# A two-layer hybrid encoder on one core: wider tiles for GLA's v, the gates' low-rank columns taken with retention's v, and another iteration for inverse roots

## The chip, the cores and the metric

The kernel runs on one core of one Trainium2 chip. The time is that of one execution on the device in microseconds, given as the median of several runs. The trace is of one execution of its own, and its terms are added up against that execution's time.

## The reference, cut to what matters

Two layers over 512 tokens of 1024 channels. In each, a normalized input h is projected to all branches at once; three mixers (retention, an S5 state space model, gated linear attention, GLA) work side by side, are gated and merged, and an MLP follows. What the change touches, from the reference:

```python
h = rmsnorm(x, norm1_g[l])
z = h @ w_in[l]
a_q, a_k, a_v, a_g, b_u, c_q, c_k, c_v, c_lr, c_r = jnp.split(z, split_idx, axis=-1)
...
ro = retention_bidir(rq, rk, a_v.reshape(Bn, L, RET_HEADS, RET_DV))
...
la_f = (jax.nn.log_sigmoid(lr @ gla_w_gate[l, 0].astype(jnp.float32)
                           + gla_b_gate[l, 0].astype(jnp.float32)) / GLA_TAU
        ).reshape(Bn, L, GLA_HEADS, GLA_DK)
...
go_f = gla_chunked(gq, gk, gv, la_f, False)
```

a_v has 256 columns (retention's v), c_v has 512 (GLA's v), and c_lr has 16, the low-rank input lr of GLA's forget gates. Inverse square roots stand in every RMSNorm and in the norms of the heads of GLA and retention.

## The kernel before, in words

Precision is kept by splitting: every float32 operand of a large matmul becomes a rounded part ("hi") and a rest ("lo"), and a product is three matmuls (hi by hi, hi by lo, lo by hi). Weights come from memory in chunks of 128 x 1024, two layers of 128 chunks; `weights` (L99) loads a chunk on SP's queue into one of three "raw" buffers, casts it on ScalarE (whi, L112) and subtracts on VectorE (wlo, L113), into a ring of five buffers. `col_tile` (L120 to L132) makes 128 output channels by 512 tokens from one chunk: 8 blocks of rows times 3 matmuls of 512 columns (L129 to L131).

h itself is not normalized before the projection: each result is scaled by the inverse root when it is evicted, as a row R over tokens or, for v, as a column r of 128 tokens.

`layer` (L311) sets the order in which the work is traced: the two u tiles of S5 (in layer 0 `u_first`, made while x arrives); `lr_proj` (L485), 16 matmuls of 512 columns that give lr with the tokens along the row; four q and k tiles of GLA, each copied twice per head by DMA ("dup", L327); the gates (`gla_gate`, L521); GLA's v by two calls of `v_tiles` (L275), each 256 columns wide; GLA's states and reads; four rotary tiles of retention (`z_tile`, `rotary`, with copies "rsw" L641 and "qfb" L672); retention's v, a third call of `v_tiles`, centred by `center` (L647); retention; then tiles of silu and merge gates, between which S5 is worked off in steps ("bg"). A step of S5 is set behind the latest product of retention's q on GpSimd (L674) and behind instructions of the tile just made (`bg_steps`). Then come the branch projections, the output projection and the MLP; at the end the last 512 tokens are done in two halves of 256, so that one half is normalized while the other is multiplied (`emit_out`).

In `v_tiles` h is the stationary side and the weights are streamed: four token tiles share two PSUM banks, and each of the 96 matmuls is 256 columns wide (L288, L290, L292). PSUM has four banks tagged "mm" (large products) and four tagged "ms" (small ones).

`rsqrt` (L134) makes an inverse root on VectorE: a shift, a multiply-add on the integer view, and three Newton steps of three instructions.

This order is not the final one: a planner takes the traced instructions, the priorities given by `hp`, the edges given by `issue_after`, a cost model and the free on-chip memory, writes each engine's queue, and chooses how many buffers a tag without a fixed count gets. Each engine then runs its queue strictly in order.

## Time and profile before

| | us |
|---|---|
| runs shown | 1573.23, 1573.24, 2206.6 |
| median | 1573.24 |
| profiled execution | 1574.72 |
| its span, first to last instruction | 1572.6 |
| TensorE busy in it | 1546.8 |

The span leaves out 2.1 us around the instructions. A line such as "PE L129 MATMUL mm<-hh,whi 128*128 128x512" is line 129's matmul with a 128 x 128 stationary side and 512 streamed columns, into the PSUM tile mm, from hh (the hi part of h) and whi. PE is TensorE, DVE VectorE, ACT ScalarE, POOL GpSimd, SP the engine that issues most DMAs. In brackets stands the engine's idle time just before, and what ended it. PEclk is the granted share of TensorE's full clock.

### The profile page before, as it was taken

What the parts mean: (1) busy time and instruction counts of PE and PEld (TensorE: products, weight loads), DVE (VectorE), ACT (ScalarE), POOL (GpSimd) and SP (SyncE); (2) the same over time, 40 slices, a digit from 0 to 9 for tenths busy, and PEclk for the clock granted to TensorE, in tenths of its full rate; (3) what the DMA queues carried; (4) which work ended last, traced back from release to release, by engine and by line L of the source; (5) the groups of instructions that cost most, each with busy time, mean ns of one, the idle gap of its engine ahead of it and who ended that gap; (6) DMA issues with size and microseconds to landing.
All of it is one profiled execution on the core that took longest, in us unless ns stands there. A gap on an engine that the chain in (4) does not pass through costs nothing.

```text
span 1572.6 us, 20692 instructions
## 1 busy us (share of the span) xinstructions
PE 1546.8 (98%) x8118; PEld 1289.1 (82%) x8118; DVE 934.1 (59%) x1583; ACT 567.8 (36%) x853; POOL 204.4 (13%) x327
## 2 busy tenths in 40 slices
PE   9999999999999999999999999999999999999997
PEld 6888877788888888888889888788888888888897
DVE  6786999855556657434548889744455434344353
ACT  5533333243433332423335324332343423232342
POOL 8242010141200000000101210102111000000002
PEclk9999999999999999999999999999999999999999
DMA  6424222233323223232434322333242223323221
GB/s 209 148 65 124 86 75 89 91 108 126 121 100 103 97 93 100 94 108 94 147 116 140 108 68 81 95 98 103 94 139 102 94 94 103 99 94 108 94 94 54
DMA packets 60512, 163.36 MB, mean 104 GB/s; under 512 B 10556, under 2 KB 17212, under 8 KB 60416
## 3 DMA queue, kind: packets, MB, share of 16 engines
q1 hardware_dynamic: 60096, 161.01, 31.5%
q8 instruction: 64, 1.05, 0.3%
q0 software_dynamic: 320, 1.05, 0.2%
q14 instruction: 32, 0.26, 0.1%
HBM read 147.11 MB, written 6.52 MB: 98 GB/s over the span
## 4 chain that ended last, share of the span: by engine, by line
PE 81%; DVE 11%; DMA 2%; issue 2%; SPq 2%; POOL 1%; ACT 1%; DVEq 0%; POOLq 0%; ACTq 0%
PE mm L129 24%; PE mm L131 24%; PE mm L130 24%; DVE wlo L113 2%; PE mm L290 1%; PE mm L292 1%; PE mm L288 1%; DMA rsw<-za 1%; DVE g L372 1%; DMA dup<-zc 1%; DMA s5y<-yscr 0%; DMA raw<-wst 0%; SPq L1111 0%; SPq L641 0%; PE ms L701 0%
## 5 line engine op out<-in xcount | busy, mean ns | idle before, releaser
L113 DVE TENSOR_TENSOR wlo<-raw,whi 128x1024 fp32r<-128x1024 f32 (+1 forms) x258 | 325.1, 1261 | 273.0 <-PE mm L130 198.2
L112 ACT CAST whi<-raw 128x1024 fp32r<-128x1024 f32 (+1 forms) x258 | 266.7, 1044 | 542.2 <-PE mm L131 437.0
L131 PE MATMUL mm<-hh,wlo 128*128 128x512 f32 x1136 | 445.9, 393 | 1.5 <-DVE wlo L113 1.5
L129 PE MATMUL mm<-hh,whi 128*128 128x512 f32 x1136 | 446.1, 393 | 0.0
L130 PE MATMUL mm<-hl,whi 128*128 128x512 f32 x1136 | 444.7, 391 | 0.0
L131 PEld LDWEIGHTS mm<-hh,wlo 128*128 128x128 f32 x1136 | 213.6, 188 | 47.8 <-DVE wlo L113 3.0
L129 PEld LDWEIGHTS mm<-hh,whi 128*128 128x128 f32 x1136 | 213.6, 188 | 45.8 <-issue 2.3
L130 PEld LDWEIGHTS mm<-hl,whi 128*128 128x128 f32 x1136 | 213.6, 188 | 44.7 <-issue 1.1
L130 PE MATMUL mm<-fl,whi 128*128 128x512 f32 (+1 forms) x576 | 210.7, 366 | 0.0
L131 PE MATMUL mm<-fh,wlo 128*128 128x512 f32 (+1 forms) x576 | 210.2, 366 | 0.0
L129 PE MATMUL mm<-fh,whi 128*128 128x512 f32 (+1 forms) x576 | 209.5, 366 | 0.0
L130 PEld LDWEIGHTS mm<-fl,whi 128*128 128x128 f32 x576 | 108.6, 189 | 17.7
L129 PEld LDWEIGHTS mm<-fh,whi 128*128 128x128 f32 x576 | 108.6, 189 | 17.7
L131 PEld LDWEIGHTS mm<-fh,wlo 128*128 128x128 f32 x576 | 108.6, 189 | 17.5
L182 POOL TENSOR_TENSOR acc<-acc,sq 128x512 f32<-128x512 f32 (+1 forms) x30 | 32.5, 1085 | 564.2 <-ACT sq L181 564.2
L118 DVE TENSOR_TENSOR fl<-ht,fh 128x512 fp32r<-128x512 f32 x64 | 44.3, 692 | 76.9 <-ACT fh L117 76.8
L446 ACT ACTIVATE ht<-ht 128x512 f32<-128x512 f32 x64 | 40.4, 631 | 86.0 <-DVE ht L445 86.0
L373 ACT ACTIVATE g<-g,cst 128x512 f32<-128x512 f32 x48 | 34.7, 724 | 88.4 <-DVE g L372 88.4
L471 DVE TENSOR_TENSOR x<-x,mm 128x512 f32<-128x512 f32 x56 | 38.3, 683 | 44.8 <-PE mm L131 44.8
L129 PE MATMUL mm<-y,whi 128*128 128x512 f32 x160 | 62.6, 391 | 0.8 <-DVE s5Y L1105 0.8
L130 PE MATMUL mm<-y,whi 128*128 128x512 f32 x160 | 62.6, 392 | 0.0
L131 PE MATMUL mm<-y,wlo 128*128 128x512 f32 x160 | 62.2, 390 | 0.0
(265 smaller groups left out, 1944.2 us busy)
## 6 DMA issues: line engine op xcount, KB each, us to landing
raw<-wst SPq DMA_DIRECT2D x254, 512.0 KB, 3.3
dup<-zc SPq DMA_DIRECT2D x32, 128.0 KB, 3.5
rsw<-za SPq DMA_DIRECT2D x32, 64.0 KB, 2.0
qfb<-za SPq DMA_DIRECT2D x16, 128.0 KB, 3.4
x<-xT SPq DMA_DIRECT2D x8, 256.0 KB, 3.6
xs<-x SPq DMA_DIRECT2D x8, 256.0 KB, 3.9
x<-xs SPq DMA_DIRECT2D x8, 256.0 KB, 3.8
outT<-out SPq DMA_DIRECT2D x8, 256.0 KB, 2.7
```

Source lines behind the costliest of these rows:

```text
L112: nc.scalar.copy(hi[:, s], raw[:, s])
L113: nc.vector.tensor_sub(lo[:, s], raw[:, s], hi[:, s].bitcast(F32))
L118: self.nc.vector.tensor_sub(lo, src, hi.bitcast(F32))
L129: nc.tensor.matmul(ps, hi[:, o:o + P], a, start=first and k == 0, stop=False)
L130: nc.tensor.matmul(ps, hi[:, o:o + P], b, start=False, stop=False)
L131: self.mmi = nc.tensor.matmul(ps, lo[:, o:o + P], a, start=False, stop=last and k == n - 1)
L182: return (eng or (nc.vector if j == KT - 1 else nc.gpsimd)).tensor_add(accs[0], accs[0], t)
L288: nc.tensor.matmul(o, a[:, s], hi[:, k * 256:(k + 1) * 256], start=f, stop=False, skip_group_check=True)
L290: nc.tensor.matmul(o, a[:, s], lo[:, k * 256:(k + 1) * 256], start=False, stop=False, skip_group_check=True)
L373: act = nc.scalar.activation(g, g, AF.Sigmoid, bias=self.smc(l, SM_BM, j))
L446: act = nc.scalar.square(t, t)
L471: ev = nc.vector.tensor_add(self.x[j], self.x[j], ps)
```

## The change

Three things are done. GLA's v is made by `v_wide`: four chunks of 256 rows by 512 columns, each token tile in a bank of its own, 96 matmuls of 512 columns. Retention's v is made by `v_lr` together with the 16 columns of lr, 272 columns in all, in two chunks of 128 x 1088, and ahead of GLA's q and k; `lr_rows` scales lr per token, splits it side by side, transposes it in four pieces and gives the gates 50 rows to contract over instead of 98. All buffers of raw and split weights become 1088 wide. Inverse roots take one Newton step and one step of third order, nine instructions in place of eleven. The host's layout of weights follows (two unused chunks are left in the numbering).

```diff
@@ -22,6 +22,8 @@
+LW = 1088
+LC = 2
@@ -105,10 +107,11 @@
             bufs = dict(bufs=5) if tag == "w" else {}
-            hi = self.sb.tile([P, CW], F32R, tag=tag, name=self.nm("whi"), **bufs)
-            lo = self.sb.tile([P, CW], F32R, tag=tag, name=self.nm("wlo"), **bufs)
+            hi = self.sb.tile([P, LW], F32R, tag=tag, name=self.nm("whi"), **bufs)
+            lo = self.sb.tile([P, LW], F32R, tag=tag, name=self.nm("wlo"), **bufs)
+            cw = self.width(c)
             for i in range(n):
-                s = slice(CW // n * i, CW // n * (i + 1))
+                s = slice(cw // n * i, cw // n * (i + 1))
                 nc.scalar.copy(hi[:, s], raw[:, s])
@@ -139,10 +142,14 @@
         u = self.small(shape, tag + "u")
-        for _ in range(3):
-            nc.vector.scalar_tensor_tensor(u, y, -0.5, y, ALU.mult, ALU.mult)
-            nc.vector.tensor_mul(u, u, v)
-            nc.vector.scalar_tensor_tensor(y, u, 1.5, y, ALU.add, ALU.mult)
+        c = math.sqrt(0.375)
+        nc.vector.scalar_tensor_tensor(u, y, -0.5, y, ALU.mult, ALU.mult)
+        nc.vector.tensor_mul(u, u, v)
+        nc.vector.scalar_tensor_tensor(y, u, 1.5, y, ALU.add, ALU.mult)
+        nc.vector.scalar_tensor_tensor(u, y, -c, y, ALU.mult, ALU.mult)
+        nc.vector.tensor_mul(u, u, v)
+        nc.vector.scalar_tensor_tensor(u, u, 1.25 / c, u, ALU.add, ALU.mult)
+        nc.vector.scalar_tensor_tensor(y, u, 1.875, y, ALU.add, ALU.mult)
         return y
@@ -231,12 +238,17 @@
+    def width(self, c):
+        return LW if LC <= c < LC + 2 else CW
-        raw = self.sb.tile([P, CW], F32, tag="raw", bufs=3, name=self.nm("raw"))
+        raw = self.sb.tile([P, LW], F32, tag="raw", bufs=3, name=self.nm("raw"))
+        cw = self.width(c)
+        src = self.io["wst"][l, c] if cw == CW else self.io["wlr"][l, c - LC]
-            s = slice(CW // n * i, CW // n * (i + 1))
-            dma = self.nc.sync.dma_start(raw[:, s], self.io["wst"][l, c][:, s])
+            s = slice(cw // n * i, cw // n * (i + 1))
+            dma = self.nc.sync.dma_start(raw[:, s], src[:, s])
@@ -272,31 +284,51 @@
-    def v_tiles(self, l, h, r):
-        nc = self.nc
-        ps = [self.mm([P, 2, 256]) for _ in range(2)]
+    def v_lr(self, l, h, r):
+        nc = self.nc
+        ps = [f([P, 272]) for f in (self.mm, self.mm, self.ms, self.ms)]
         for half in range(2):
             for tt in range(4):
-                o = ps[tt // 2][:, tt % 2, :]
+                s = slice(tt * P, (tt + 1) * P)
                 for k in range(4):
                     a, b = h[half * 4 + k]
-                    s = slice(tt * P, (tt + 1) * P)
-                    f = half == 0 and k == 0 and tt % 2 == 0
-                    e = half == 1 and k == 3 and tt % 2 == 1
-                    nc.tensor.matmul(o, a[:, s], hi[:, k * 256:(k + 1) * 256], start=f, stop=False,
-                                     skip_group_check=True)
-                    nc.tensor.matmul(o, a[:, s], lo[:, k * 256:(k + 1) * 256], start=False, stop=False,
-                                     skip_group_check=True)
-                    nc.tensor.matmul(o, b[:, s], hi[:, k * 256:(k + 1) * 256], start=False, stop=e,
-                                     skip_group_check=True)
+                    wh, wl = (w[:, k * 272:(k + 1) * 272] for w in (hi, lo))
+                    nc.tensor.matmul(ps[tt], a[:, s], wh, start=half == 0 and k == 0, stop=False)
+                    nc.tensor.matmul(ps[tt], a[:, s], wl, start=False, stop=False)
+                    nc.tensor.matmul(ps[tt], b[:, s], wh, start=False, stop=half == 1 and k == 3)
         out = []
+        lr = self.slot(shape=(P, 4, 16), s="lr")
         with self.hp(15000):
                     out.append(self.slot(shape=(P, 2, 256), s="v"))
-                nc.scalar.activation(out[-1][:, tt % 2, :], ps[tt // 2][:, tt % 2, :], AF.Copy, scale=r[:, tt:tt + 1])
+                rr = r[:, tt:tt + 1]
+                nc.scalar.activation(out[-1][:, tt % 2, :], ps[tt][:, 0:256], AF.Copy, scale=rr)
+                nc.scalar.activation(lr[:, tt, :], ps[tt][:, 256:272], AF.Copy, scale=rr)
+        return out, lr
+    def v_wide(self, l, h, r):
+        nc = self.nc
+        ps = [self.mm() for _ in range(4)]
+        for c in range(4):
+            hi, lo = self.weights(l)
+            for tt in range(4):
+                s = slice(tt * P, (tt + 1) * P)
+                for k in range(2):
+                    a, b = h[2 * c + k]
+                    wh, wl = (w[:, k * 512:(k + 1) * 512] for w in (hi, lo))
+                    nc.tensor.matmul(ps[tt], a[:, s], wh, start=c == 0 and k == 0, stop=False)
+                    nc.tensor.matmul(ps[tt], a[:, s], wl, start=False, stop=False)
+                    nc.tensor.matmul(ps[tt], b[:, s], wh, start=False, stop=c == 3 and k == 1)
+        out = []
+        with self.hp(15000):
+            for tt in range(4):
+                out.append(self.slot(s="v"))
+                nc.scalar.activation(out[-1], ps[tt], AF.Copy, scale=r[:, tt:tt + 1])
         return out
@@ -315,7 +347,8 @@
         us = [self.u_tile(l, h, R, ps) for ps in pu]
-        lrT = self.lr_proj(l, h, R)
+        av, lr = self.v_lr(l, h, r)
+        lrT = self.lr_rows(l, lr)
         qd, kd = [], []
@@ -328,7 +361,7 @@
             gl = [self.gla_gate(hd, lrT, qd[hd], kd[hd]) for hd in range(4)]
-        cv = [self.v_tiles(l, h, r) for _ in range(2)]
+        cv = self.v_wide(l, h, r)
         if l == 0:
@@ -350,7 +383,7 @@
                     lst.append(self.rotary(z, cs, sn))
-        av = self.center(self.v_tiles(l, h, r))
+        av = self.center(av)
         with self.hp(8000):
@@ -482,40 +515,31 @@
-    def lr_proj(self, l, h, R):
+    def lr_rows(self, l, lr):
         nc, io = self.nc, self.io
-        with self.hp(20000):
-            raw = self.slot(s="wlr")[:, 0:KT * 16].rearrange("p (k c) -> p k c", c=16)
-            with self.tc.issue_after(self.wdma.ins):
-                nc.sync.dma_start(raw, io["wlr"][l])
-            w = self.sb.tile([P, KT, P], F32R, tag="w", bufs=5, name=self.nm("wlrs"))
-            nc.gpsimd.memset(w.bitcast(F32), 0.0)
-            self.wcp = nc.scalar.copy(w[:, :, 0:16], raw)
-            nc.vector.tensor_sub(w[:, :, 16:32], raw, w[:, :, 0:16].bitcast(F32))
-        ps = self.mm()
-        for k in range(KT):
-            nc.tensor.matmul(ps, w[:, k, :], h[k][0], start=k == 0, stop=False)
-            nc.tensor.matmul(ps, w[:, k, :], h[k][1], start=False, stop=k == KT - 1)
         lrT = self.slot(F32R, s="lrT")
         with self.hp(15000):
-            t = self.slot(s="lrt")
-            nc.vector.tensor_mul(t[0:32, :], ps[0:32, :], R[0:32, :])
-            nc.scalar.copy(lrT[0:32, :], t[0:32, :])
-            nc.vector.tensor_sub(lrT[32:64, :], t[0:32, :], lrT[0:32, :].bitcast(F32))
-            self.lrc = nc.scalar.copy(lrT[64:96, :], t[0:32, :])
-            with self.tc.issue_after(self.uev.ins):
-                nc.vector.memset(lrT[96:128, :].bitcast(F32), 1.0)
+            t = self.slot(shape=(P, 4, 64), s="lrt")
+            nc.gpsimd.memset(t[:, :, 48:64], 1.0)
+            tr = t.bitcast(F32R)
+            nc.scalar.copy(tr[:, :, 0:16], lr)
+            nc.vector.tensor_sub(tr[:, :, 16:32], lr, t[:, :, 0:16])
+            nc.scalar.copy(tr[:, :, 32:48], lr)
+            ps = self.ms()
+            for tt in range(4):
+                nc.tensor.transpose(ps[0:64, tt * P:(tt + 1) * P], t[:, tt, :], self.ident)
+            self.lrc = nc.scalar.copy(lrT[0:64, :], ps[0:64, :])
             raw = self.slot(s="wgr")
             with self.tc.issue_after(self.wdma.ins):
-                nc.sync.dma_start(raw[0:98, :], io["wg"][l])
+                nc.sync.dma_start(raw[0:50, :], io["wg"][l])
                 nc.sync.dma_start(self.scm, io["tab"][:, T_SC:T_SC + 512])
             hi = self.slot(F32R, s="wgh")
-            with self.tc.issue_after(self.wcp.ins):
-                nc.scalar.copy(hi[0:98, :], raw[0:98, :])
-            nc.vector.scalar_tensor_tensor(self.wg[0:98, :], hi[0:98, :].bitcast(F32), self.cst[0:98, C_M:C_M + 1],
-                                           raw[0:98, :], ALU.mult, ALU.add)
+            nc.scalar.copy(hi[0:50, :], raw[0:50, :])
+            nc.vector.scalar_tensor_tensor(self.wg[0:50, :], hi[0:50, :].bitcast(F32), self.cst[0:50, C_M:C_M + 1],
+                                           raw[0:50, :], ALU.mult, ALU.add)
         return lrT
@@ -523,7 +547,7 @@
         ps = self.ms()
-        nc.tensor.matmul(ps, self.wg[0:98, hd * P:(hd + 1) * P], lrT[0:98, :], start=True, stop=True)
+        nc.tensor.matmul(ps, self.wg[0:50, hd * P:(hd + 1) * P], lrT[0:50, :], start=True, stop=True)
         a = self.slot(s="a")
@@ -568,8 +592,7 @@
         nc.vector.copy_predicated(sT, self.cst[:, C_MB:C_MB + P].bitcast(U32).unsqueeze(1).to_broadcast([P, 4, P]), psb)
-        c0 = (hd % 2) * P
-        v = [cv[hd // 2][n // 2][:, n % 2, c0:c0 + P] for n in range(4)]
+        v = [x[:, hd * P:(hd + 1) * P] for x in cv]
         psk = self.ms([P, 4, P])
...
@@ -1149,11 +1172,10 @@
+        ch += [np.zeros((P, CW), f)] * 2
-        halves = lambda c: [blk(w[512 * i:512 * i + 512], c, 256) for i in range(2)]
-        ch += halves(1792) + halves(2048)
+        ch += [blk(w[256 * i:256 * i + 256], 1792, 512) for i in range(4)]
-        ch += halves(512)
```

## Rows read from the trace of the kernel before

**Rows 1.** The page's part 1: busy us of an engine, share of the span, instructions

```profile
PE 1546.8 (98%) x8118; PEld 1289.1 (82%) x8118; DVE 934.1 (59%) x1583; ACT 567.8 (36%) x853; POOL 204.4 (13%) x327
```

**Rows 2.** What TensorE waited for: us in total, times, longest

```profile
PE ms L168 <- DVE dg L166: 3.0, 1, 3.0
PE mm L131 <- DVE wlo L113: 2.1, 3, 0.9
PE ms L666 <- DVE za L644: 1.9, 1, 1.9
PE m L1101 <- DVE s5S L1080: 1.7, 1, 1.7
...
PE mm L288 <- DVE sT L570: 1.4, 1, 1.4
PE ms L959 <- DVE W L948: 1.4, 1, 1.4
```

**Rows 3.** TensorE's timeline in layer 0: start, us, line, tiles

```profile
27.51 0.39 PE L129 MATMUL mm<-hh,whi 128*128 128x512 f32 x1
...
32.72 0.39 PE L131 MATMUL mm<-hh,wlo 128*128 128x512 f32 x1
...
51.12 0.28 PE L288 MATMUL mm<-whi,hh 128*128 128x256 f32 x1
...
54.84 0.28 PE L290 MATMUL mm<-wlo,hh 128*128 128x256 f32 x1
```

**Rows 4.** Stretches: us, busy us of PE, PEld, DVE, ACT, POOL, PEclk, DMA

```profile
119.10:155.00 35.90, 33.16 (x228) 29.45 (x226) 21.61 (x36) 12.13 (x20) 6.89 (x9) 1.00 0.43 128
155.00:301.40 146.40, 143.81 (x902) 114.63 (x902) 136.22 (x300) 50.09 (x76) 20.16 (x31) 1.00 0.26 83
...
936.50:941.00 4.50, 4.50 (x20) 3.80 (x17) 3.58 (x15) 0.00 (x0) 0.00 (x0) 0.54 0.23 90
```

**Rows 5.** TensorE's timeline in layer 1, around lr_proj and four transposes

```profile
804.76 0.39 PE L497 MATMUL mm<-hh,wlrs 128*128 128x512 f32 x1
...
808.39 0.39 PE L129 MATMUL mm<-hh,whi 128*128 128x512 f32 x1
...
836.59 0.60 PE L558 MATMUL ms<-cst,dup 128*128 128x128 f32 x4
...
837.14 0.28 PE L288 MATMUL mm<-whi,hh 128*128 128x256 f32 x1
```

**Rows 6.** GLA's q and k copies: VectorE's timeline, the tile's issues and landing

```profile
50.91 0.69 DVE L545 TENSOR_TENSOR dup<-dup,cum 128x512 f32<-128x512 f32 x1 [0.76 <-ACT cum L543]
...
L327 SPq DMA_DIRECT2D dup<-zc x32: 467/594/935, 38.7 to 838.9; - x32
...
DMA to landing us min/median/max: 2.2/3.5/5.6
```

**Rows 7.** Timelines of ScalarE and of VectorE, start of layer 0

```profile
21.56 1.99 ACT L112 CAST whi<-raw 128x1024 fp32r<-128x1024 f32 x2 [2.88 <-PE mm L740]
...
24.04 2.52 DVE L113 TENSOR_TENSOR wlo<-raw,whi 128x1024 fp32r<-128x1024 f32 x2
```

**Rows 8.** Timelines of VectorE and of TensorE, end of the kernel

```profile
1563.20 0.16 DVE L143 SCALAR_TENSOR_TENSOR nu<-ny 128x2 f32<-128x2 f32 x1
...
1563.79 0.16 DVE L143 SCALAR_TENSOR_TENSOR nu<-ny 128x2 f32<-128x2 f32 x1
...
1565.00 0.90 PE L168 MATMUL ms<-dg,cst 128*128 128x256 f32 x2 [3.03 <-DVE dg L166]
```

**Rows 9.** Timelines of TensorE and GpSimd, layer 0, from retention's v on

```profile
119.10 0.40 PE L288 MATMUL mm<-whi,hh 128*128 128x256 f32 x2
...
134.39 0.40 PE L129 MATMUL mm<-hh,whi 128*128 128x512 f32 x1
...
154.96 2.52 POOL L674 TENSOR_TENSOR qfb<-qfb,cst 128x512 f32<-128x512 f32 x2 [20.20 <-DMA qfb<-za]
```

More of the change, by code (lines that the diff above doesn't have):

```diff
@@ L1133, in _layout @@
     wst = np.empty((depth, NCH, P, CW), f)
-    wlr = np.empty((depth, P, KT, 16), f)
-    wg = np.empty((depth, 98, 512), f)
+    wlr = np.empty((depth, 2, P, LW), f)
+    wg = np.empty((depth, 50, 512), f)
     s5bc = np.empty((depth, 2, P, 2, 2, 8, 16), f)
@@ L1172, in _layout @@
             wst[l, i] = c
-        wlr[l] = w[:, 2304:2320].reshape(KT, P, 16).transpose(1, 0, 2)
+        vlr = np.concatenate([w[:, 512:768], w[:, 2304:2320]], 1)
+        for i in range(2):
+            wlr[l, i] = blk(vlr[512 * i:512 * i + 512], 0, 272)
         gw, gb = A("gla_w_gate")[l], A("gla_b_gate")[l]
         gl = gw.reshape(2, 16, 4, 64).transpose(1, 2, 0, 3).reshape(16, 512)
-        wg[l, 0:96] = np.tile(gl, (6, 1))
-        wg[l, 96:98] = gb.reshape(2, 4, 64).transpose(1, 0, 2).reshape(512)
+        wg[l, 0:48] = np.tile(gl, (3, 1))
+        wg[l, 48:50] = gb.reshape(2, 4, 64).transpose(1, 0, 2).reshape(512)
         for i, (br, cr) in enumerate((("s5_b_re", "s5_c_re"), ("s5_b_im", "s5_c_im"))):
@@ L1204, in _layout @@
     cst[:, C_MB:C_MB + P] = i[:, None] > i[None, :]
-    cst[64:96, C_M] = cst[97, C_M] = -1.0
+    cst[32:48, C_M] = cst[49, C_M] = -1.0
     for hd in range(4):
```

## The prediction

> **What bounds the kernel now.** I read the page's busy times first [rows 1]: TensorE is busy for 1546.8 of 1572.6 us, VectorE for 934.1. A busy TensorE need not be at its peak, so I next listed what it waited for [rows 2]. The longest entry is 3.0 us, at the very end; the next are 1 to 2 us each. So almost the whole span is TensorE's own queue of matmuls, and a change is worth what it does to that queue, unless it opens a new wait. Third I read the pace, since a matmul's printed duration (0.39 us) overlaps the next one's: only the distance between starts counts. With 512 columns, 24 matmuls of one tile start between 27.51 and 32.72, 23 steps, 0.2265 us each; with 256 columns, 32 matmuls start between 51.12 and 54.84, 31 steps, 0.120 us each [rows 3]. Two narrow ones thus cost 0.240, one wide one 0.2265: a fixed part of about 13 ns per matmul is what widening can save. Last I looked where another engine is close to being the bound: between the last rotary tile of layer 0 (119.1) and the read of its S5 states (301.4), VectorE is busy for 21.6 of 35.9 and then for 136.2 of 146.4 us [rows 4].
>
> **Part 1, GLA's v in 512 columns.** Per layer 192 matmuls of 256 columns go (two calls of v_tiles, 96 each: three lines, four token tiles, eight blocks of rows of h), 192 x 0.120 = 23.04 us; 96 of 512 come, 96 x 0.2265 = 21.74. Gain 1.30 us per layer, all on TensorE's queue. Weight bytes, casts and splits stay the same. Four accumulators of one bank now fill all four "mm" banks for 22 us, and no head of GLA gets its v before the end of it, where heads 0 and 1 had theirs half-way. TensorE fills that time with v_wide itself and then the four rotary tiles, so I cost it at nothing; by the nearest rows, waits of the heads' mask copies [rows 2], it could be 1.4 us either way.
>
> The Trainium skill (TensorE: Matmul & The Clock Gate, Back-to-back issue gap) gives the warm step as columns / 2.4 GHz plus about 2.5 ns. By it, as an estimate, a layer's part 1 would save only 96 x 2.5 ns = 0.24 us, and the whole sum below would be 2.1 us smaller: 1567.9 in place of 1565.8. The rows show five times that fixed part in this kernel, and the measurement decides.
>
> **Part 2, the low-rank columns.** lr_proj's 16 matmuls of 512 columns go: from 804.76 to the next tile's start at 808.39, 3.63 us [rows 5]. Its memset, cast and split were done ahead and cost nothing now. In exchange, retention's 96 matmuls grow from 256 to 272 columns: between the two paces a column costs (0.2265 - 0.120) / 256 = 0.42 ns, so 96 x 16 x 0.42 ns = 0.64 us. Four transposes of 64 columns come; the nearest row is four of GLA's 128-column transposes between v matmuls, which push the second matmul behind them from 0.12 to 0.55 us after their start: 0.43 us [rows 5]. The width is the stationary side's, so I keep 0.43. The gates' four matmuls contract over 50 rows instead of 98 but still stream 512 columns: no change. Net gain 3.63 - 0.64 - 0.43 = 2.56 us per layer.
>
> VectorE loses the scaling, the split into lrT and the memset of lr and gets a smaller split and the new root's share; ScalarE gets four more evictions of 16 columns and one of the transposes. All of it stands beside the q and k tiles.
>
> **Part 3, the move.** Retention's v (two weight chunks, 48 matmuls each) now stands ahead of the four q and k tiles of GLA. Its loads on SP (512 KB each and 32 KB more for lr, whose own load of 64 KB goes) come first too, ahead of those tiles' loads and of the sixteen duplicating copies, which slip with their tiles. The q and k tiles start 96 x 0.1267 - 3.63 = 8.5 us later against the start of the layer. In layer 0 the first head's product comes at 50.91 [rows 6]. Its two tiles would now run from 27.5 + 8.5 = 36.0 to 36.0 + 48 x 0.2265 = 46.9; four copies of 0.59 us to issue and 3.5 us to land [rows 6] make it 52.8 at the earliest, 2 us late. Behind it TensorE has v_wide, which needs none of this, so I cost it at nothing; if GLA's heads end 2 us late, the rotary tiles are still in front of their readers.
>
> At layer 0's start something is uncovered. lr_proj's weights came early, and its matmuls, which by their 3.63 us began near 23.9 and ended at 27.51, hid the next chunk's cast (from 21.56, held by the u tiles, which kept the weight buffers) and its split, which began at 24.04 and took 1.26 us [rows 7]. Now that chunk is needed at 23.9 itself. Bounds: nothing, if its cast uses the buffer that lr_proj held and goes early, and 24.04 + 1.26 - 23.9 = 1.4 us, if the order stays. I take the middle, 0.7 us; in layer 1 the chunks stream and it is nothing.
>
> The buffers of weights grow from 1024 to 1088 columns, all of them. That takes on-chip memory from other tiles' buffer counts. Bounds: nothing, and a doubling of TensorE's present waits for splits, 2.1 us [rows 2]; I take nothing, as these waits are rare.
>
> **Part 4, the roots.** Eleven VectorE instructions become nine. There are 18 roots (six of norm_stats, eight of gla_read, four of retention), at 0.197 us a step (1563.20 to 1563.79 is three), so 0.39 us each and 7.1 us of VectorE in all. Only the last one is on TensorE's path: TensorE idles 3.03 us for it before 1565.00 [rows 8]. Gain 0.39 us; what is late next there is the same chain, two steps shorter. The other 17 stand beside matmuls.
>
> **The sum.** Two layers x (1.30 + 2.56) = 7.72, plus 0.39, less 0.7: 7.4 us. The profiled execution took 1574.72 us (its span and 2.1 us around it), so 1567.3; the median of the runs shown is 1.5 us under it, so I predict 1573.24 - 7.4 = 1565.8 us. That is 0.5%, well inside the 2% that a measurement of this kernel can tell from no change.
>
> **Rivals.**
>
> A, the waits of layer 0 go as well. Retention's v is now evicted and centred long before it is wanted, so its centring and two weight splits leave VectorE's queue where the rotary and S5 chains are late. The waits there, 1.9 (rotated k), 1.7 (S5 state) and 1.4 (S5 weights), sum to 5.0 us [rows 2]; in layer 1 a stretch of 4.5 us in the midst of retention ran at a granted clock of 0.54, so near the lower level, 1.2 GHz [rows 4], and may gain up to 2 us more. For it: all of these end on VectorE. Against it: the order of each queue is planned anew, and such waits appear where the plan mistimes, not where work is most. Time 1565.8 - 5.0 = 1560.8.
>
> B, slower: the move takes away S5's cover. S5's first load stands on GpSimd behind the last product of retention's q, which ended at 154.96 + 2.52 = 157.5, 38.4 us after the last rotary tile; 15.3 of these TensorE spent from 119.10 to 134.39, mostly on retention's v [rows 9]. If that chain keeps its 38.4 us while the silu tiles begin at once, S5 starts 15.3 us later against its reader, which already waits 1.7 us. VectorE's idle time in the dense stretch is 10.2 us [rows 4]; if it makes up none, all or half of that, the wait grows by 15.3, 5.1 or 10.2 us. Layer 1 has S5's tables ready and is counted as nothing. Time 1565.8 + 10.2 = 1576.0, slower than before. It decides once the slip, less what idle time recovers, is over 7.4 us. Against it: GpSimd sat idle for 20.2 us of that chain, waiting for copies [rows 9], and these can be issued earlier.
>
> C, layer 0's gain is lost: in its dense stretch VectorE sets the time, so TensorE's 3.86 us there turn into waits, and only layer 1 and the end gain. Time 1573.24 - 3.86 - 0.39 + 0.7 = 1569.7. For it: 93% busy [rows 4]. Against it: VectorE sheds work in layer 0's mixers too (7 roots x 0.39 = 2.7 us, and lr's instructions).
>
> That the change does not do what it says, with TensorE's 8118 records unchanged, I give nothing.
>
> **How the numbers follow.** Forecast 0.55, C 0.18, B 0.14, A 0.13. The forecast's own ends are its unknowns: start 0.7 either way, heads 1.4 either way, memory 0 to 2.1, so 1563.7 to 1570.0. The range for 8 in 10 takes in A and C and the near part of B (5.1 us: 1570.9, and somewhat over it): 1559.5 to 1575. Nearly all of every case is within 2% (1541.8 to 1604.7): same 0.97. Faster by over 2% would need 24 us that no row shows, 0.01; slower by over 2% would need a collapse of S5's cover in both layers, 0.02.
>
> **What would show it.** Right: TensorE's records fall by 216 (192 + 32 matmuls fewer, 8 transposes more); wide v matmuls start 0.2265 us apart and 272-column ones 0.127; no wait for lr before the gates; the last root's wait at 2.6 instead of 3.0 us. S5's load on GpSimd under 25 us after the first silu tile says C or better; over 30 says B. Wrong: TensorE idle time growing by more than 4 us between the rotary tiles and S5's read, or a granted clock under 1.0 in a new place.

## The result, and the profile of the changed kernel

The changed kernel takes 1582.87 us (median of five runs, 1579.1 to 1586.13) against 1573.24: a ratio of 1.0061, 95% interval 1.005 to 1.0072. It is 0.6% slower, where 0.5% faster had been forecast; the 7.4 us of the sum are missing and 9.6 us stand on the other side. The run of 2206.6 us of the kernel before lies far from all others and is left out of the ratio. Its profiled execution has a span of 1580.9 us, 8.3 more than before.

The busy times of the page, to be read against [rows 1]:

```profile
PE 1548.1 (98%) x7902; PEld 1278.9 (81%) x7902; DVE 919.1 (58%) x1541; ACT 579.1 (37%) x853; POOL 199.7 (13%) x327
```

TensorE has 216 instructions fewer, as forecast, and VectorE 15 us less to do. Yet TensorE's busy time is 1.3 us higher, where the sum took more than 7 us off its queue: busy time counts a matmul at the lower clock as busy for longer. What TensorE waited for, its list of waits (us in total, times, longest), to be read against [rows 2]:

```profile
PE ms L689 <- DVE za L667: 4.2, 2, 2.3
PE ms L739 <- DVE rS L734: 2.9, 4, 1.3
PE ms L648 <- DVE rS L734: 2.7, 1, 2.7
...
PE ms L175 <- DVE dg L173: 2.5, 1, 2.5
...
PE mm L300 <- DVE wlo L116: 1.1, 1, 1.1
```

The first three are new in size: L689 transposes retention's k and waits for its rotary product (1.9 us, once, before), L739 reads retention's states, L648 transposes GLA's results. Together 9.8 us, all on VectorE, all around retention. The wait for the last root is 0.5 us shorter, as forecast.

Where the time went shows in stretches. Layer 1's mixers of before, from the first matmul of lr_proj to the middle norm (columns as in [rows 4]):

```profile
804.76:1224.98 420.22, 417.83 (x2349) 351.36 (x2348) 274.42 (x433) 157.54 (x244) 62.63 (x70) 0.99 0.33 104
...
932.00:944.00 12.00, 11.00 (x77) 9.65 (x74) 10.83 (x34) 1.00 (x2) 0.08 (x2) 0.72 0.14 45
```

The same of the changed kernel, and its stretches of lower clock; a further one, in the last 9 us, the kernel before has too:

```profile
803.75:1232.22 428.47, 419.18 (x2238) 347.31 (x2237) 266.27 (x415) 158.99 (x244) 63.03 (x70) 0.98 0.32 102
...
148.00:156.00 8.00, 7.79 (x44) 6.46 (x45) 7.74 (x25) 2.14 (x6) 3.52 (x8) 0.79 0.32 98
912.00:924.00 12.00, 10.41 (x59) 8.40 (x57) 5.98 (x14) 3.21 (x5) 2.48 (x2) 0.72 0.41 111
...
940.00:952.00 12.00, 11.87 (x59) 10.71 (x60) 10.08 (x25) 2.00 (x4) 3.05 (x4) 0.57 0.14 45
```

Layer 1's mixers are 8.3 us longer, where 3.9 shorter was forecast: 12.1 us off. TensorE idles 428.47 - 419.18 = 9.3 us there against 2.4 before, 6.9 more. And its granted clock costs, by the length of a stretch times the share of the clock that is missing, 12 x 0.28 + 12 x 0.43 = 8.5 us against 12 x 0.28 = 3.4 us, 5.2 more. At the lower of the two levels, 1.2 GHz, full-width matmuls start 0.427 us apart (11 steps from 916.28 to 920.97) instead of 0.2265. The two terms make 12.1. In layer 0 the middle norm comes at 454.58 instead of 456.26, a gain of 1.7 where 3.2 was forecast; a new stretch of lower clock (8 x 0.21 = 1.7 us) is of that size. The remaining 1.7 us of the 8.3 lie in the MLPs and the end (0.7 in layer 0, 1.1 in layer 1, half of that one wait for ScalarE at 1526.89) and were not followed up. So the time went into waits around retention, and nearly as much again into matmuls run at the lower clock behind those waits.

### The profile page after: what moved, and what is told of

The parts are those of the page before. It is cut to its first block, busy times and chain, and to the rows that moved or that the text cites. A ratio compares the mean times of both kernels' runs of the same rounds, so it can differ in the third digit from the quotient of the medians.

```text
span 1580.9 us, 20380 instructions
## 1 busy us (share of the span) xinstructions
PE 1548.1 (98%) x7902; PEld 1278.9 (81%) x7902; DVE 919.1 (58%) x1541; ACT 579.1 (37%) x853; POOL 199.7 (13%) x327
## 4 chain that ended last, share of the span: by engine, by line
PE 70%; DVE 4%; issue 4%; DMA 2%; POOL 1%; ACT 0%; SPq 0%; DVEq 0%; POOLq 0%; ACTq 0%
PE mm L132 22%; PE mm L133 22%; PE mm L134 22%; DMA raw<-wst 1%; DVE wlo L116 1%; PE mm L324 0%; DMA rsw<-za 0%; POOL s5c L1097 0%; PE mm L326 0%; PE mm L325 0%; SPq L664 0%; DVE st L608 0%; PE ms L175 0%; DVE za L667 0%; PE ms L166 0%
## 5 line engine op out<-in xcount | busy, mean ns | idle before, releaser
L116 DVE TENSOR_TENSOR wlo<-raw,whi 128x1024 fp32r<-128x1024 f32 (+2 forms) x258 | 317.8, 1233 | 403.6 <-issue 196.5
L115 ACT CAST whi<-raw 128x1024 fp32r<-128x1024 f32 (+2 forms) x258 | 269.8, 1048 | 651.4 <-PE mm L134 591.5
L134 PE MATMUL mm<-mh,wlo 128*128 128x512 f32 x128 | 49.7, 391 | 1.3 <-DVE wlo L116 1.3
```

The costliest lines, as they stand in the source:

```text
L115: nc.scalar.copy(hi[:, s], raw[:, s])
L116: nc.vector.tensor_sub(lo[:, s], raw[:, s], hi[:, s].bitcast(F32))
L134: self.mmi = nc.tensor.matmul(ps, lo[:, o:o + P], a, start=False, stop=last and k == n - 1)
```

## The experiments

Every run stands beside runs of the kernel before on the same chip; the ratios are to those. Medians of different groups of runs are compared more loosely: the kernel before alone moves by 1.8 us from group to group. The first theory (T, cover) fell at once; what replaced it is tested further down.

### Four kernels: the move alone, no move, a filler, another order

move_only, against the kernel before:

```diff
         lrT = self.lr_proj(l, h, R)
+        av = self.v_tiles(l, h, r)
         qd, kd = [], []
...
-        av = self.center(self.v_tiles(l, h, r))
+        av = self.center(av)
```

> The kernel before, with one edit: retention's v is made (in 256 columns, as before) right after lr_proj instead of behind the rotary tiles. Nothing of TensorE's work is saved. Theory T (cover): retention's v was the work without dependencies that stood where the chains of retention and S5 are late; taken from there, layer 1 shows about 7 us more of waits and 5 us more at the lower clock, layer 0 some 1 to 2 us: 1582 to 1590 us. Theory W (the wide v, all four heads' v only at its end, is at fault): no change, 1571.5 to 1575. Theory N (each edit makes a new plan of the queues, and this one came out badly by chance): within 4 us of 1573 on either side.

Measured: 1568.63 us, ratio 0.9964 (0.995 to 0.9978). Faster by 0.36%, so T fell, and the move by itself is no cause of the loss. W's and N's numbers missed as well, on the fast side. Its trace shows rival A of the prediction. Layer 0 from 24 us to its middle norm:

```profile
24.00:449.00 425.00, 421.36 (x2425) 350.74 (x2424) 320.65 (x594) 160.49 (x262) 103.40 (x180) 1.00 0.34 107
```

TensorE idles 3.6 us there; before it was 432.00 - 422.47 = 9.5 from 24.00 to its middle norm at 456.00. The waits of layer 0 that rival A names go or shrink.

no_move, against the kernel before:

```diff
-        cv = [self.v_tiles(l, h, r) for _ in range(2)]
+        cv = self.v_wide(l, h, r)
```

and the new rsqrt. 

> The kernel before, with GLA's v in 512 columns and the new roots, but lr_proj and retention's v where they were. T: the gains of parts 1 and 4 come, 1573.24 - 2 x 1.30 - 0.39 = 1570.3 (1568.5 to 1572). W: the loss stays, 1580 or more, with the waits for za and rS in retention. N: within 4 us of 1570 on either side.

Measured: 1579.07 us, ratio 1.0029 (1.0018 to 1.004). A loss is here without any move: 7.9 us over roots_only below, which is this kernel without the wide v. W was right in direction, 0.9 us short of its number. The waits are others than W named; the longest is the wide v's own, for splits of its weights:

```profile
PE mm L318 <- DVE wlo L113: 7.4, 2, 6.2
```

filler, against the changed kernel:

```diff
+        ps = [self.mm([P, 2, 256]) for _ in range(2)]
+        for i in range(96):
+            nc.tensor.matmul(ps[i // 48][:, i // 24 % 2, :], h[i % 8][0][:, i // 24 * P:i // 24 * P + P],
+                             self.lw[0][:, i % 4 * 256:i % 4 * 256 + 256], start=i % 48 == 0, stop=i % 48 == 47,
+                             skip_group_check=True)
         av = self.center(av)
```

> The changed kernel with 96 matmuls of 256 columns per layer added where retention's v had stood, on data that is there already and with a result that nobody reads: 2 x 96 x 0.120 = 23.0 us of matmuls more. T: the waits for za and rS (9.8 us in both layers) fall under 3 us and the lower clock of layer 1 goes back to the one stretch of before, so of the 23.0 us some 12 to 15 are given back: 1591 to 1595. W and N: nothing is given back, 1582.9 + 23.0 = 1605.9, or over 1602.

Measured: 1599.83 us, ratio 1.0158 (1.0143 to 1.0173), so 17 us more than the changed kernel; 6 of the 23 are given back, between the two theories. Cover counts for something, but not for most of the loss.

rot_first: the loop over the four rotary tiles goes ahead of `cv = self.v_wide(l, h, r)`.

> The changed kernel with retention's four rotary tiles ahead of GLA's wide v, so that the 96 wide matmuls (21.7 us) stand behind the rotary tiles; no work is added or left out. T: cover is back in the place where it lacked, so the sum of the prediction comes, 1565.8 (1563 to 1569). W: GLA's heads get their v later still, so 1583 or more. N: anywhere between 1568 and 1584.

Measured: 1583.67 us, ratio 1.0059 (1.0044 to 1.0074). T failed again; W's number came, and it lies within N's range too. Here too the wide v's wait for its splits is the longest (6.8 us).

### What is wrong with the wide v: structure, width, or late gates

narrow: the changed kernel with `cv = [self.v_tiles(l, h, r) for _ in range(2)]` and the reader's indices of before.

> The changed kernel with GLA's v made as before, by two calls of v_tiles in 256 columns; retention's v with the low-rank columns stays ahead of q and k, and the new roots stay. Theory S (the structure of the wide v: no head gets its v before all 96 matmuls are through, so the heads' work is pushed behind it and the rotary tiles are used up as its cover): the loss goes, 1568.6 of move_only less 2 x 2.56 (low-rank columns) less 0.4 (roots) plus 0.7 (start) = 1563.8 (1561 to 1567). Theory L (the low-rank columns come too late, so the gates begin at 50.1 instead of 38.8 us): the loss stays, 1578 or more.

Measured: 1568.83 us, ratio 0.9967 (0.9956 to 0.9979). 14.0 us under the changed kernel, so the wide v carries the loss; 5 us over the number of S and outside its range, which is taken up below.

wide_move:

> move_only with GLA's v in 512 columns and the new roots; lr_proj stays, so the gates are early. S: the loss stays although the gates are early, 1575 to 1588, with waits in retention. L: 1568.6 - 2 x 1.30 - 0.4 = 1565.6 (1563 to 1568).

Measured: 1590.46 us, ratio 1.0105 (1.009 to 1.012). The loss comes with early gates too, a little over S's range: L fell as the cause of it. This kernel is no_move with retention's v moved, and it is 11.4 us slower than no_move. So the move, which gains 5.8 us by itself, costs 11.4 us beside the wide v: the two are not independent, and why is not settled.

cut_in_two, against the changed kernel:

```diff
-                    nc.tensor.matmul(ps[tt], a[:, s], wh, start=c == 0 and k == 0, stop=False)
...
+                    for q in range(2):
+                        o, e = slice(q * 256, q * 256 + 256), c == 3 and k == 1 and q == 1
+                        nc.tensor.matmul(ps[tt][:, o], a[:, s], wh[:, o], start=c == 0 and k == 0 and q == 0,
+                                         stop=False, skip_group_check=True)
...
```

> The changed kernel with each of the 96 wide matmuls of GLA's v cut into two of 256 columns, in the same banks and order and with the same evictions at the end. S: the loss stays and the narrow pace is paid on top, 1582.9 + 2 x 1.30 = 1585.5 (1582 to 1589). Theory X (the wide matmul itself is at fault, its pace or what it does to the granted clock): the loss goes, 1564 to 1570.

Measured: 1579.22 us, ratio 1.0034 (1.0021 to 1.0047). It has narrow's 192 matmuls of 256 columns, and is 10.4 us slower than narrow: X fell, the structure is at fault. But it is 3.7 us faster than the changed kernel where S had 2.6 slower, under S's range too; why is not settled. Its stretch of lower clock in layer 1 costs more than any other between the start and the end of these traces, 22 x 0.39 = 8.6 us:

```profile
916.00:938.00 22.00, 19.92 (x113) 16.60 (x111) 17.35 (x48) 5.42 (x9) 4.17 (x7) 0.61 0.12 38
```

roots_only: the kernel before with the new rsqrt.

> The kernel before with the new roots alone. All theories: 0.4 us less at the end of the kernel, and nothing else, so 0.4 us under the kernel before (within 1 us of it). Theory N (any edit makes a new plan, with gains and losses by chance): more than 2 us away from it on either side.

Measured: 1571.2 us, ratio 0.9987 (0.9977 to 0.9996): 2.6 us by the medians, 0.6 to 3.6 by the interval. More than the 0.4 at the end, and by the median past the 2 us that N had set as its sign; the interval reaches on both sides of it.

### The version that beats both, and a miss

move_roots: move_only with the new rsqrt.

> move_only with the new roots; lr_proj stays, GLA's v stays in 256 columns. If the roots give what roots_only gave (2.6 us, of which 0.4 at the end and the rest as shorter waits): 1566.0 (1564.5 to 1567.3), and then the low-rank columns of the run narrow, whose matmuls are 5.1 us less, cost 2 to 3 us instead of gaining 5. If the roots are worth only the 0.4 us of the end here: 1568.2.

Measured: 1564.34 us, ratio 0.9943 (0.993 to 0.9957): the fastest so far, 0.6% faster than before. The roots give more here than at the end of the kernel.

wide_between: v_wide between the two passes of the loop that makes GLA's q and k.

> The changed kernel with GLA's wide v between the first two and the last two of GLA's q and k tiles, so that heads 0 and 1, which need only the first two, have their v some 11 us earlier against the gates, and the last two q and k tiles stand behind it as cover. S (no head gets its v before the whole of the wide v is through, and that is late against the gates): most of the loss of 14 us against narrow goes, 1566 to 1574. Theory B (the wide v is at fault by itself, by its four banks held together or its evictions all at once): the loss stays, 1579 to 1587.

Measured: 1591.46 us, ratio 1.0118 (1.0102 to 1.0133). S's number missed, and B's range lies below it as well. But the edit made the last two q and k tiles later, and with them heads 2 and 3: their last read came at 134 us in layer 0, against 126 in the changed kernel. That suggested theory O, which looks at the last head instead of the first: in the kernels with the loss GLA's last head ends behind the start of retention, in those without it well ahead.

### Theory O: the two chains meet on VectorE

TensorE's timeline of move_roots in layer 0: the last head's last read (L598) and retention's first transposes (L671).

```profile
116.14 0.39 PE L598 MATMUL ms<-st,dup 128*128 128x128 f32 x2
...
130.93 0.60 PE L671 MATMUL ms<-cst,za 128*128 128x128 f32 x4
```

The same two of the changed kernel (L616, L689), and the transposes of the second pair of heads:

```profile
122.96 0.60 PE L689 MATMUL ms<-cst,za 128*128 128x128 f32 x4
...
126.02 0.39 PE L616 MATMUL ms<-st,dup 128*128 128x128 f32 x2
...
134.96 0.43 PE L739 MATMUL ms<-rS,qfb 128*128 128x64 f32 x2 [1.26 <-DVE rS L734]
...
138.82 0.48 PE L134 MATMUL mm<-hh,wlo 128*128 128x512 f32 x1
...
148.21 0.63 PE L689 MATMUL ms<-cst,za 128*128 128x128 f32 x4 [1.84 <-DVE za L667]
```

14.8 us ahead in the one, 3.1 us behind in the other. What the meeting does shows in VectorE's timeline of the changed kernel, ahead of that last wait:

```profile
132.77 0.16 DVE L623 TENSOR_SCALAR ss<-ss 128x4 f32<-128x4 f32 x1
...
136.96 0.23 DVE L734 SCALAR_TENSOR_TENSOR rS<-rS,ms 64x64 f32<-64x64 f32 x1
...
137.61 0.69 DVE L625 TENSOR_TENSOR go<-go,ny 128x512 f32<-128x512 f32 x1
138.22 1.22 DVE L116 TENSOR_TENSOR wlo<-raw,whi 128x1024 fp32r<-128x1024 f32 x1
139.47 0.69 DVE L284 TENSOR_TENSOR za<-mm,R 128x512 f32<-128x512 f32 x1
144.46 0.69 DVE L666 TENSOR_TENSOR za<-za,cos 128x512 f32<-128x512 f32 x1 [4.30 <-DMA rsw<-za]
...
146.33 1.74 DVE L667 TENSOR_TENSOR za<-za,rsw 128x512 f32<-128x512 f32 x1 [0.58 <-POOL rsw L665]
```

From 132.77 to 138.22 the last head's root and scaling (L623 to L625) and the small steps of retention's first pair (L734) take turns on VectorE. Retention's reads on TensorE (L739) wait for these steps, 1.8 us in two waits, and the last matmul of the last rotary tile (138.82) stands behind them in TensorE's queue. So that tile is evicted only at 139.47. Its copies land 4.3 us later, and TensorE waits at 148.21; the lower clock of 148 to 156 follows. The next four runs test O.

silu_ahead, against the changed kernel:

```diff
+        sa = [self.silu_tile(l, h, R) for _ in range(2)]
         aq, ak = [], []
...
+            if sa:
+                return sa.pop(0)
             sw = self.silu_tile(l, h, R)
```

> The changed kernel with the first two of the six silu tiles ahead of the rotary tiles (10.9 us of matmuls without dependencies between GLA's heads and retention); no work is added or left out. Theory O (the last heads of GLA still run when retention begins, 126.4 against 123.0 us in layer 0 and 903.2 against 899.7 in layer 1, and both chains meet on VectorE): the overlap goes and most of the loss with it, 1566 to 1574. Theory B (the wide v is at fault by itself, its four banks or its evictions all at once): the loss stays, 1580 to 1586.

Measured: 1575.05 us, ratio 1.0012 (1.0002 to 1.0022). Retention begins at 141.20, the last head ends at 124.34: the overlap is gone, and 7.8 us of the loss with it. That is 1 us over O's range and well under B's.

silu_ahead_mr, the same edit on move_roots:

> move_roots with the first two silu tiles ahead of the rotary tiles, the control for silu_ahead. There GLA's last head ends 13 to 15 us before retention begins, so O says that nothing is to be had: 1562 to 1568. If silu tiles ahead are of use by themselves, it gains as much as silu_ahead does.

Measured: 1575.37 us, ratio 1.0008 (0.9999 to 1.0018). That is 7 us over O's range: the edit has a price of its own. It costs 11 us where there is no overlap (8.4 us more of TensorE's idle time, 4.7 of them waits for S5's steps, which lose two tiles to stand behind) and gains 7.8 where there is one. Without the overlap the two kernels, one with the wide v and the low-rank columns, one with neither, come out 0.3 us apart. That the price is the same in both is not shown.

late_v:

> move_roots with the evictions of the first half of GLA's v set behind the last matmul of the second half; every matmul, its width, its order in the program and the number of evictions stay. S and O: the four heads are worked off behind the whole of v, the last of them ends at or behind the start of retention, and 5 to 15 us come on top of 1564.3: 1570 to 1580. B: nothing to speak of, 1563 to 1567.

Measured: 1563.41 us, ratio 0.9933 (0.9918 to 0.9948). The edge did not move the evictions (74.11 us in layer 0, 74.60 in move_roots), so this tells nothing on lateness; it is move_roots in a second order of the queues, with the same time.

narrow_late, against move_roots:

```diff
+        ps = [self.mm() for _ in range(4)]
+        for q in range(2):
+            for half in range(2):
+                hi, lo = self.weights(l)
+                for tt in range(4):
+                    o = ps[tt][:, q * 256:q * 256 + 256]
...
+            for tt in range(4):
+                out.append(self.slot(s="v"))
+                nc.scalar.activation(out[-1], ps[tt], AF.Copy, scale=r[:, tt:tt + 1])
```

> move_roots with the two narrow halves of GLA's v gathered side by side in the four banks that the wide v would take, and evicted in four pieces of 512 columns at the end; the 192 matmuls of 256 columns, their order and the weight chunks stay. S and O: the four heads are worked off behind the whole of v, the last of them ends at or behind the start of retention, and the time rises from 1564.3 by 8 to 20 us, to 1572 to 1585. If the width of the matmuls is what counts: 1563 to 1567.

Measured: 1577.86 us, ratio 1.0025 (1.0015 to 1.0036). 13.5 us more, with every matmul and weight chunk the same. TensorE's timeline of it in layer 0 (L693 retention's transposes, L620 the last head's read):

```profile
124.42 0.60 PE L693 MATMUL ms<-cst,za 128*128 128x128 f32 x4
...
131.42 0.39 PE L620 MATMUL ms<-st,dup 128*128 128x128 f32 x2
```

Its two longest waits of TensorE, both in retention and on VectorE (L742 reads retention's masked scores):

```profile
PE ms L742 <- DVE rsT L720: 3.7, 3, 1.5
PE ms L693 <- DVE nu L144: 3.0, 2, 1.5
```

The last head ends 7.0 us behind the start of retention, as S and O say. Holding GLA's v back to the end, in four banks, is enough to bring the loss, without a wide matmul. The run does not part the lateness from the four banks; but neither its list of waits nor that of the changed kernel has TensorE waiting for an eviction of v to free a bank, and silu_ahead keeps both and gives back 7.8 us.

O's sign holds in the traces of all 18 kernels. In the eight that take 1577.86 us or more, the last head's last read starts between 8.7 us behind and 0.1 us ahead of retention's first transposes; in the ten that take 1575.4 us or less, it starts 12.0 us or more ahead. How far the two overlap does not set how large the loss is (7.0 us in narrow_late at 1577.86, 3.1 in the changed kernel at 1582.87). Nor is the meeting around retention the only way to the loss: in no_move and rot_first the longest wait is that of the wide v for its own splits. So it is shown that v held back as a whole brings the loss; the path by retention is shown in the changed kernel and narrow_late, and not in each of the eight.

### Why the low-rank columns bring nothing

narrow is 4.5 us slower than move_roots, though it has 5.1 us less of matmuls. lr_both puts lr_proj ahead of v_lr again; wide_bufs changes three sizes in move_roots:

```diff
-            hi = self.sb.tile([P, CW], F32R, tag=tag, name=self.nm("whi"), **bufs)
+            hi = self.sb.tile([P, CW + 64], F32R, tag=tag, name=self.nm("whi"), **bufs)
...
```

> The run narrow with lr_proj put back ahead of v_lr: retention's v is still made in 272 columns, four banks and buffers of 1088, but the gates take lr from lr_proj, early; the 16 extra columns are not read. Theory G (the gates begin some 10 us later in narrow, and what the matmuls save is waited for behind them): 1564.3 of move_roots plus 2 x 0.64 for the extra columns, 1565.6 (1563.5 to 1568). Theory V (v_lr by itself, its banks and evictions, is at fault): narrow plus 2 x 2.56, 1573 to 1575.

Measured: 1571.12 us, ratio 0.9981 (0.9972 to 0.999): between G and V.

> move_roots with all buffers of raw and split weights 1088 wide, of which 1024 are used. If the memory that they take costs nothing, as the prediction had it: 1564.3 (1563 to 1566). If it costs buffers elsewhere: 1567 or more, and then part of narrow's loss is theirs.

Measured: 1569.27 us, ratio 0.997 (0.9958 to 0.9981). The unused 64 columns cost 4.9 us by the medians, 4.2 by the ratios. The traces of the two kernels have the same instructions in nearly the same order (SP's is the same); what differs is whom one load waits for. In move_roots it is ScalarE, in wide_bufs VectorE.

SP's timeline of move_roots in layer 1, and of wide_bufs behind it:

```profile
907.13 0.53 SPq L243 DMA_DIRECT2D raw<-wst  x1
907.77 2.42 SPq L677 DMA_DIRECT2D qfb<-za  x4
```

```profile
912.91 0.33 SPq L243 DMA_DIRECT2D raw<-wst  x1
913.34 2.67 SPq L677 DMA_DIRECT2D qfb<-za  x4
```

In wide_bufs the load goes out the moment a split on VectorE ends (911.59 + 1.29 = 912.88), and retention's copies of q stand behind it on SP, 5.6 us later than in move_roots. GpSimd's product of these copies then falls on S5's steps on VectorE. Timelines of move_roots, GpSimd and VectorE:

```profile
912.55 2.52 POOL L679 TENSOR_TENSOR qfb<-qfb,cst 128x512 f32<-128x512 f32 x2 [2.12 <-DMA qfb<-za]
...
917.75 0.68 DVE L1068 TENSOR_TENSOR s5a<-s5a,s5b 128x512 f32<-128x512 f32 x1
918.35 0.68 DVE L1069 TENSOR_TENSOR s5e<-s5e,s5c 128x512 f32<-128x512 f32 x1
```

and of wide_bufs:

```profile
917.94 3.49 POOL L679 TENSOR_TENSOR qfb<-qfb,cst 128x512 f32<-128x512 f32 x2 [6.14 <-DMA qfb<-za]
...
919.11 1.19 DVE L1068 TENSOR_TENSOR s5a<-s5a,s5b 128x512 f32<-128x512 f32 x1
920.23 1.76 DVE L1069 TENSOR_TENSOR s5e<-s5e,s5c 128x512 f32<-128x512 f32 x1
```

The same two VectorE instructions take 2.95 us instead of 1.36. TensorE then waits 1.2 us for a mask product that move_roots does not wait for (L720 for rsT), and the clock falls. The stretch around it in wide_bufs, and the like stretch of move_roots:

```profile
926.00:938.00 12.00, 10.18 (x71) 9.35 (x72) 11.33 (x32) 2.05 (x3) 0.98 (x3) 0.72 0.14 44
```

```profile
922.00:934.00 12.00, 9.51 (x93) 8.37 (x93) 11.33 (x31) 2.26 (x4) 2.09 (x4) 1.00 0.13 44
```

In that stretch the lower clock costs 12 x 0.28 = 3.4 us in wide_bufs and nothing in move_roots, which idles there even longer (2.5 against 1.8 us). So most of the price of the buffers is clock. move_roots shows how near a thing that is: three of its five executions took 1562.8 to 1564.3 us at a mean granted clock of 0.997 or 0.998, the other two 1567.2 and 1567.6 us at 0.994, where the executions of wide_bufs stand (0.993 and 0.994).

At equal buffers, narrow is only 0.4 us under wide_bufs where its matmuls are 5.1 us less. Against lr_both, which differs from it only in where lr comes from, it has 2 x (3.63 - 0.43) = 6.4 us less and gains 2.3. So v_lr does no harm by itself (lr_both is 1.9 over wide_bufs, 1.3 of it the extra columns), and some 4 of the 6.4 us are lost where lr comes late: G fits that part, though no wait was traced to it.

## Why the prediction was wrong, point by point

**Part 1, the step that failed.** "TensorE fills that time with v_wide itself and then the four rotary tiles, so I cost it at nothing", with 1.4 us either way as bounds. The size of the matmuls was right: in layer 1 the wide v took 24.18 us from 840.22 to 864.40 with 1.87 of other matmuls between, so 22.3 for 96, 0.232 each. What failed is the cost of nothing for the lateness of the heads' v: narrow_late puts it at +13.5 us, and narrow against the changed kernel at 14.0. In narrow the last evictions of v start at 80.6 us for heads 0 and 1 and at 98.0 for heads 2 and 3, in the changed kernel at 88.7 for all. Two heads get theirs 8 us later, two 9 us earlier; but the heads are worked off one after another, so the first sets the chain, and the last read moves from 116.4 to 126.1. The reasoning looked at what TensorE does meanwhile. It did not ask where the heads' chain ends, and what else stands on VectorE then. The nearest rows for a bound were one mask copy, not the chain of four heads against retention's start. The formula that the prediction takes from the Trainium skill (TensorE: Matmul & The Clock Gate, Back-to-back issue gap) is given there for a matmul by itself, and for a stream of weight loads and matmuls, the section says, it counts too little at small widths and too much at large ones. The rows of this kernel's stream show 0.2265 us at 512 columns, more than the formula's 0.216; the sum did not use it.

**Part 2.** The matmuls fell as worked out: 96 of 272 columns, four transposes in, lr_proj out. The path did not: at equal buffers 0.4 of 5.1 us came. "No wait for lr before the gates" held in the trace, but what the matmuls saved was waited for later.

**Part 3, the move.** Forecast 0, with 0.7 at the start; the wait at the start was 1.1, inside its bounds. The move by itself gains 5.8 us (move_only), the 5.0 of rival A and a little more: rival A's mechanism was right for it and had 0.13. Beside the wide v the same move costs 11.4 us (wide_move against no_move), which no rival had. Rival B is refuted in this kernel: S5's load on GpSimd stands at 149.15, 10.0 us after the first silu tile begins (139.14), where over 30 was to say B, and S5's states are read in layer 0 at 295.39, earlier than before (303.5). C came out the other way round: it had layer 0's gain lost and layer 1's kept, but layer 0 gained 1.7 us and layer 1 lost 8.3.

**The buffers.** "I take nothing, as these waits are rare", bound 2.1. Measured 4.9 in move_roots, over the bound, since the bound counted waits for splits and the price came by SP's queue and the clock.

**Part 4.** The last wait shrank by 0.5, as forecast (0.4). "The other 17 stand beside matmuls" was too strict: 2.6 us in the kernel before and 4.3 between move_only and move_roots by the medians (3.3 by the ratios, whose intervals overlap).

**The sum.** By the runs: move -5.8, roots -4.3, buffers +4.9, low-rank columns -0.4, wide v +14.0, in all +8.4; measured +9.6. By the ratios the same steps are -5.7, -3.3, +4.2, -0.5 and +14.8, in all +9.5. This holds for one order of adding the parts; in another the move and the wide v have other prices. Of the prediction's two alarms, a granted clock under 1.0 in a new place went off in both layers. More than 4 us of new idle time went off in layer 1 (6.9 us); in layer 0 TensorE idles 7.0 us from 119.10 to 303.50 before and 7.1 us from 117.00 to 295.40 now. What it lacked was a rival in which the wide v itself is slower.

**What stays open.** Why cut_in_two is 3.7 us faster than the changed kernel with more work, and why the wide v costs 7.9 us without the move (no_move against roots_only), 14 beside the low-rank columns and 26 on move_roots (wide_move). v_lr in buffers of 1024 was not tried. Theory N, that each edit's new plan brings gains and losses by chance, is not ruled out for the small terms (roots, buffers, low-rank columns). Against it for the large one: all eight kernels with the loss have GLA's v held back as a whole, and of the ten others only silu_ahead has.

## What to carry to other kernels

Where an engine is 98% busy, widening its instructions is priced by what waits for their result, not by their pace: ask when the last consumer's chain ends and which chain begins then on the next engine. Making one result late as a whole (four banks evicted at the end instead of two and two) cost five times what the wider instructions saved (13.5 us against 2 x 1.3). Do the parts of such a change one at a time, and then in pairs: here the move and the roots alone were 0.6% faster, two further edits that also shorten TensorE's queue buried that, and the move that gains by itself costs time beside the wide v.

## What was not expected of the hardware

In layer 1 of the changed kernel the lower clock takes nearly as much (5.2 us more) as the waits ahead of it (6.9 more), and it falls on the full-width matmuls behind them. Summed over windows of 4 us whose granted clock is under 0.97, the last stretch of each kernel left out, it costs 0 in move_roots and move_only, 3.4 us in the kernel before, 10.2 in the changed kernel, 13.6 in cut_in_two and 15.2 in wide_move. Whether a given wait brings it is a near thing: wide_bufs and move_roots idle alike there, and only one falls; in layer 1 of the changed kernel waits of 0.65 and 0.51 us (911.12 and 913.40) stand ahead of a fall, and one of 2.31 us (925.23) brings none. The Trainium skill (TensorE: Matmul & The Clock Gate, HAM oscillation) says that waits for DMA between short bursts of matmuls send the array back to the lower clock and leave the next burst cold. The traces agree in that the falls of the changed kernel, and the one of the kernel before (932.00), stand at waits, here waits for VectorE on an engine that is 98% busy; that each wait brings a fall they do not show.

A VectorE instruction with both inputs in on-chip memory took 1.19 and 1.76 instead of 0.68 us while GpSimd multiplied (L1068, L1069 above), and GpSimd's pair took 3.49 instead of 2.52. In the whole trace of wide_bufs, of VectorE's TENSOR_TENSOR instructions on 128x512 tiles without a PSUM input, the 113 that none of GpSimd's overlaps take 0.71 us at most, and of the 32 that one overlaps 12 take 1.19 to 1.80. The Trainium skill (SBUF — State Buffer, SBUF: two separate sides) says that such an instruction and one of GpSimd take one port pair in turn, each for its whole length; these rows agree: the four instructions need 3.88 us one after another by their shorter times, and here they end 4.05 us after the first starts.
